# One store of a DMA-bound batched matrix product cut into eight uneven parts

## Chip, cores, metric

The kernel runs on one core of a Trainium2 chip. The metric is the device time of one execution in microseconds (us), lower is better. A "ratio" below is the mean time of one kernel's fast runs over the mean of the fast runs of the kernel before that are recorded with it, so it is not quite the ratio of the medians quoted beside it.

## The reference

```python
# x: 32 x 256 x 512, y: 32 x 512 x 384, float32
def reference(x, y):
    return np.einsum('bij,bjk->bik', x, y).astype(np.float32)
```

In and out together are 54.5 MB, read and written once.

## The kernel before

Batches go in pairs: 16 units u of two batches. Per unit the kernel loads y (two DMAs of 128 rows of 6 KB) and, every second unit, x (128 rows of 16 KB); it transposes x on TensorE, rounds both to float16, multiplies, copies the result to SBUF and stores it with one DMA of 128 rows of 6 KB. All 56 DMAs are issued by SyncE (SP) on one queue.

```python
def store(u):
    keep(nc.sync.dma_start(
        out=out[u * G : (u + 1) * G].rearrange("g (m e) k -> (g m) e k", e=NE),
        in_=o_of.pop(u),                    # tile [128, 4, 384] float32
    ))

for s in range(U + 2):                      # U = 16 units
    if s + ahead < U: load(s + ahead)       # ahead = 2
    # ... (transposes of the first x)
    if s >= 2:        collect(s - 2)        # PSUM -> SBUF copies on ACT and DVE
    if 1 <= s <= U:   multiply(s - 1)
    if s < U:         round_y(s)
    # ... (transposes of the next x)
    if s >= 2:        store(s - 2)
```

`keep` holds the issues in this order on SP. The DMAs take eight completion semaphores in turn, called lanes below: the reports in the trace of the kernel before fall on eight semaphores, 112 on each, 16 for each of seven DMAs. A lane is used again eight DMAs later, and the issue of that DMA waits until the earlier one has landed: the load issued at 104.27 us came 0.02 us after the store of 86.46, eight DMAs before it, had landed. In the kernel's source there is no trace of this: it stands in the instruction list and in the waits of the profile.

## Time and profile before

| | before |
|---|---|
| median of 3 runs | 135.97 us |
| span of the profiled run | 134.3 us |
| DMA queue, share of 16 engines | 97.8% |
| issues of stores 11, 12, 13, 14, 15 | 111.2, 115.9, 123.7, 126.5, 129.1 us |
| last landing | 129.08 + 4.4 = 133.4 us |

Landings are the times at which the 16 DMA engines report to a DMA's semaphore. The trace has each, without the engine's number (the views print only the last of the 16; the others are read from the packed trace itself). Store 11 is reported between 124.03 and 126.00 us, so the engines are up to 2 us apart by then.

The following two views of the kernel before are for comparison with later ones: the DMA view of 124 to 135 us, in 40 slices of 0.275 us, busy share in tenths and GB/s; and the stretch sums (span, busy time of PE, PEld, DVE, ACT and POOL, then clock, DMA share, GB/s).

```profile
DMA  9999999999999999999868999999743100000000
GB/s 425 425 402 402 469 380 439 425 402 425 380 380 469 425 380 447 402 425 402 335 268 335 425 402 447 447 380 402 291 201 156 75 0 0 0 0 0 0 0 0
```

```profile
124.00:125.90 1.90, 1.90 (x27) 1.65 (x24) 1.15 (x4) 1.90 (x6) 0.00 (x0) 1.00 1.04 426
```

The engines are full until 129.2, a few wait for store 15 in three slices, and from slice 28 (131.7) they run dry one by one. Store 12, the one that the change cuts, moves in the first half of this view, at 426 GB/s.

### The profile page before, as it was taken

What the parts mean: (1) busy time and instruction counts of PE and PEld (TensorE: products, weight loads), DVE (VectorE), ACT (ScalarE), POOL (GpSimd) and SP (SyncE); (2) the same over time, 40 slices, a digit from 0 to 9 for tenths busy, and PEclk for the clock granted to TensorE, in tenths of its full rate; (3) what the DMA queues carried; (4) which work ended last, traced back from release to release, by engine and by line L of the source; (5) the groups of instructions that cost most, each with busy time, mean ns of one, the idle gap of its engine ahead of it and who ended that gap; (6) DMA issues with size and microseconds to landing.
All of it is one profiled execution on the core that took longest, in us unless ns stands there. A gap on an engine that the chain in (4) does not pass through costs nothing.

```text
span 134.3 us, 1968 instructions
## 1 busy us (share of the span) xinstructions
PE 88.5 (66%) x768; PEld 73.2 (55%) x768; DVE 56.2 (42%) x128; ACT 63.9 (48%) x129; POOL 0.7 (1%) x6
## 2 busy tenths in 40 slices
PE   0049494979299767786099771976439986597920
PEld 0049474768177666666078661864427665476810
DVE  0004717471743365711634318460363425628620
ACT  3004837662762476712744428560475336738610
POOL 2000000000000000000000000000000000000000
PEclk9999999999959999999968999999965899779997
DMA  5999999999999999999999999999999999999993
GB/s 112 415 400 450 409 417 421 456 388 421 417 448 408 409 428 421 457 394 417 413 443 436 408 417 428 442 422 402 425 423 444 426 402 427 419 427 419 417 394 158
DMA packets 8073, 54.65 MB, mean 407 GB/s; under 512 B 896, under 2 KB 896, under 8 KB 7040
## 3 DMA queue, kind: packets, MB, share of 16 engines
q1 hardware_dynamic: 8064, 54.53, 97.8%
q8 instruction: 6, 0.10, 0.3%
q14 instruction: 3, 0.02, 0.0%
HBM read 41.94 MB, written 12.58 MB: 406 GB/s over the span
## 4 chain that ended last, share of the span: by engine, by line
DMA 78%; PE 13%; ACT 4%; DVE 0%; issue 0%
DMA y_sb<-in_y_dram 40%; DMA x_sb<-in_x_dram 38%; PE o_ps L130 9%; PE t_ps L99 3%; ACT xt_sb L107 2%; ACT y_r L116 1%; ACT o_sb L143 1%; DVE o_sb L145 0%
## 5 line engine op out<-in xcount | busy, mean ns | idle before, releaser
L130 PE MATMUL o_ps<-y_r,xt_sb 128*64 128x384 f16 x512 | 52.4, 364 | 28.5 <-ACT o_sb L143 20.8
L130 PEld LDWEIGHTS <-xt_sb 128*64 128x64 f16 x512 | 39.1, 121 | 38.8 <-issue 22.4
L116 ACT CAST y_r<-y_sb 128x384 f16<-128x384 f32 x64 | 29.5, 514 | 38.7 <-DMA y_sb<-in_y_dram 38.6
L99 PE MATMUL t_ps<-identity,x_sb 128*128 128x128 f32 x256 | 36.9, 301 | 11.4 <-DMA x_sb<-in_x_dram 11.4
L99 PEld LDWEIGHTS t_ps<-identity,x_sb 128*128 128x128 f32 x256 | 34.1, 211 | 16.0 <-issue 16.0
L118 DVE CAST y_r<-y_sb 128x384 f16<-128x384 f32 x64 | 20.0, 356 | 46.7 <-DMA y_sb<-in_y_dram 46.7
L107 ACT CAST xt_sb<-t_ps 128x512 f16<-128x512 f32 x32 | 22.4, 731 | 23.6 <-PE t_ps L99 23.6
L105 DVE CAST xt_sb<-t_ps 128x512 f16<-128x512 f32 x32 | 22.6, 728 | 24.1 <-PE t_ps L99 23.8
L145 DVE COPY o_sb<-o_ps 128x384 f32<-128x384 f32 x32 | 16.3, 544 | 2.1 <-PE o_ps L130 2.1
L143 ACT COPY o_sb<-o_ps 128x384 f32<-128x384 f32 x32 | 13.9, 492 | 1.3 <-PE o_ps L130 1.3
L107 ACT ACT_TABLE_LOAD x1 | 1.3, 1283 | 0.7 <-PEq L192 0.7
masks.py:199 POOL TENSOR_SCALAR_AFFINE_SELECT identity<-identity 128x128 f32<-128x128 f32 x1 | 0.3, 294 | 0.1
masks.py:197 POOL MEMSET identity<- 128x128 f32 x1 | 0.2, 206 | 0.3 <-POOLq L192 0.3
L192 POOL MEMSET const-bfloat16-1.0<- 128x1 bf16 x1 | 0.1, 102 | 0.0
L192 POOL MEMSET const-uint8-127<- 128x1 uint8 x1 | 0.1, 102 | 0.0
L192 POOL MEMSET const-float32-0.0<- 128x1 f32 x1 | 0.1, 99 | 0.2 <-issue 0.2
L192 POOL MEMSET const-float32-1.0<- 128x1 f32 x1 | 0.1, 99 | 0.0
## 6 DMA issues: line engine op xcount, KB each, us to landing
y_sb<-in_y_dram SPq DMA_DIRECT2D x32, 768.0 KB, 17.9
x_sb<-in_x_dram SPq DMA_DIRECT2D x8, 2048.0 KB, 20.8
out_dram<-o_sb SPq DMA_DIRECT2D x16, 768.0 KB, 17.8
```

The source lines that it names most:

```text
L99: nc.tensor.transpose(t_ps[:, f, h], x_sb[:, h * NE + e + f, t::NJ], identity)
L105: keep(nc.vector.tensor_copy(dst, t_ps))
L107: keep(nc.scalar.copy(dst, t_ps))
L116: keep(nc.scalar.copy(yr_of[u][:, g, t], y_sb[:, g, t]))
L118: keep(nc.vector.tensor_copy(yr_of[u][:, g, t], y_sb[:, g, t]))
L130: nc.tensor.matmul(o_ps[g * M : (g + 1) * M], xt_sb[:, t, e, a * PQ : (a + 1) * PQ].rearrange("c p h -> c (p h)"), y_r[:, g, t], start=(t ...
L143: keep(nc.scalar.copy(o_of[u][:, e], ps_of[u][e]))
L145: keep(nc.vector.tensor_copy(o_of[u][:, e], ps_of[u][e]))
L192: nc = _bacc.Bacc("TRN2", target_bir_lowering=False, num_devices=1)
```

## The change

The intent: engines that are late at the end should get fewer rows of one store, early ones more. An unsplit store gives eight to each (eight packets between two reports of an engine, in the kernel before).

```diff
+PARTS = (0, 64, 76, 88, 100, 112, 120, 124, 128)
 ...
     def store(u):
-        keep(nc.sync.dma_start(out=..., in_=o_of.pop(u)))
+        o_sb = o_of.pop(u)
+        dst = out[u * G : (u + 1) * G].rearrange("g (m e) k -> (g m) e k", e=NE)
+        cuts = PARTS if u == U - 4 else (0, P)
+        for k, m in enumerate(cuts[:-1]):
+            rows = slice(m, cuts[k + 1])
+            keep(nc.sync.dma_start(out=dst[rows], in_=o_sb[rows]))
```

(The removed call is shortened.)

More of the change, by code (lines that the diff above doesn't have):

```diff
@@ L148, in store @@
     def store(u):
-        keep(
-            nc.sync.dma_start(
-                out=out[u * G : (u + 1) * G].rearrange("g (m e) k -> (g m) e k", e=NE),
-                in_=o_of.pop(u),
-            )
-        )
+        o_sb = o_of.pop(u)
[4 more added lines that the diff above has]
+            keep(nc.sync.dma_start(out=dst[rows], in_=o_sb[rows]))
     ahead = LAG - 2
```

## The prediction

> **What bounds the kernel now.** I read the page first (the DMA row of the slices, the queue table, the chain of waits), then the waits and the timeline of the engine that issues the DMAs (SP), then the DMA view and the stretch sums of the last ten microseconds.
>
> ```profile
> DMA  5999999999999999999999999999999999999993
> ...
> q1 hardware_dynamic: 8064, 54.53, 97.8%
> ...
> DMA 78%; PE 13%; ACT 4%; DVE 0%; issue 0%
> ```
>
> The first line is the mean busy share of the 16 DMA engines in 40 slices: full from the second slice to the last but one. The second says that the one hardware queue's packets fill 97.8% of 16 engines' span. The third says that the chain that ended last is 78% DMA. PE is busy 66% of the span, ACT 48%, DVE 42%, so the bound is the transport of 54.5 MB, and only the edges can be bettered: time in which some DMA engine is without work. At the end there is some. The sums of three late stretches (columns: span, busy time of PE, PEld, DVE, ACT, POOL, then clock, DMA share, GB/s):
>
> ```profile
> 129.50:130.10 0.60, 0.00 (x0) 0.00 (x0) 0.00 (x0) 0.00 (x0) 0.00 (x0) 1.00 0.74 307
> 130.10:131.50 1.40, 0.00 (x0) 0.00 (x0) 0.00 (x0) 0.00 (x0) 0.00 (x0) 1.00 1.03 426
> 131.50:134.30 2.80, 0.00 (x0) 0.00 (x0) 0.00 (x0) 0.00 (x0) 0.00 (x0) 0.71 0.24 97
> ```
>
> Compute has ended. From 129.5 to 130.1 a quarter of the engines idle, and after 131.5 the share is 0.24. The DMA view of 128.5 to 134.3, with slices of 0.145 us, has the shape:
>
> ```profile
> DMA  8989887759999999999999764535200000000000
> ```
>
> The dip in slices 7 to 9 (129.5 to 129.95) is engines that have ended the last store but one and wait for the last one. From slice 22 (131.7) they run dry one after another until slice 30 (132.9). So the 16 engines are not level: the first is about 1.2 us ahead of the last. That unevenness is what the change goes for. If the engines ended together, the end would come earlier by the unused time after 131.5, that is (132.95 - 131.5) - 0.24 x 2.8 = 0.78 us, plus the dip, 0.26 x 0.6 = 0.16 us: an estimate of 0.9 us at most, 0.7% of the time.
>
> The end itself is set by the last stores. The timeline of the issuing engine in narrow windows, one line each (start, duration, what):
>
> ```profile
> 96.91 0.34 SPq L150 DMA_DIRECT2D out_dram<-o_sb  x1
> 98.71 0.33 SPq L81 DMA_DIRECT2D y_sb<-in_y_dram  x1
> 109.28 0.33 SPq L81 DMA_DIRECT2D y_sb<-in_y_dram  x1
> 111.22 0.34 SPq L150 DMA_DIRECT2D out_dram<-o_sb  x1
> 115.90 0.34 SPq L150 DMA_DIRECT2D out_dram<-o_sb  x1
> 123.67 0.33 SPq L150 DMA_DIRECT2D out_dram<-o_sb  x1
> 126.49 0.33 SPq L150 DMA_DIRECT2D out_dram<-o_sb  x1
> 129.08 0.33 SPq L150 DMA_DIRECT2D out_dram<-o_sb  x1
> ```
>
> The last five are stores 11 to 15 (of 0 to 15). The DMA view gives the time from issue to landing as 14.8, 11.9, 6.0, 5.0 and 4.4 us, so they land at 126.0, 127.8, 129.7, 131.5 and 133.45: 1.83 us apart, the pace of the engines, 0.23 us for one 6 KB row. Store 12 has about ten microseconds of queued work ahead of it. And the waits of the issuing engine:
>
> ```profile
> SPq L150 <- DVE o_sb L145: 20.3, 5, 7.1
> SPq L150 <- DMA y_sb<-in_y_dram: 16.7, 11, 1.6
> SPq L81 <- DMA out_dram<-o_sb: 7.2, 5, 1.4
> ```
>
> A store that waits for a load of y, and a load of y that waits for a store, share no data. The program's instruction list explains it: DMAs take eight completion semaphores in turn ("lanes"), and each issue waits until the DMA eight places earlier has landed. The trace agrees: the load issued at 104.27 came 0.02 us after the store of 86.46, eight DMAs before it, landed (17.8 us later). In the tail this binds nothing today: stores 12 to 15 wait on lanes that came free at 113.0 (issued at 95.02, 18.0 to landing), 114.9, 116.7 and 118.6, long before their data was ready. It is the number that the change disturbs.
>
> [...]the issue at 129.08 ending the dip at about 129.95, 0.8 to 0.95 us.[...]
>
> **The change, part by part.** Removed: one issue of 128 rows. Added: eight issues of 64, 12, 12, 12, 12, 8, 4 and 4 rows, same bytes. On PE, ACT, DVE and POOL the instruction lists are unchanged.
>
> [...]
>
> *Issue time.* Seven more issues by 0.34 us are 2.4 us of SP, which has 7.1 us without work between 116 and 123.67: hidden in themselves.
>
> *Lanes.* This is the part that I think decides. The eight parts take all eight lanes once, and each must wait for what its lane held. Part 0: 115.90. Part 1: lane free at 114.9, issue 116.3. Part 2: 116.7. Part 3: 118.6. Part 4 waits for store 10 (issued 102.46, 18.0): 120.45. Part 5 waits for the y load of 104.27: 122.3. Part 6 waits for the last load (109.28 + 14.8): 124.1. Part 7 waits for store 11: 126.0. Store 13 then takes the lane of part 0. Part 0 stands behind store 11 on every engine, so its last engine ends four rows later: 126.0 + 4 x 0.23 = 126.92. So store 13 goes out at 126.95 and not at 123.67, 3.3 us later, although its data lie ready. Store 14 follows 0.4 us later, store 15 at 129.08 as now.
>
> *What this does to the engines.* Ahead of store 13 they have only store 11 and the parts. The packets of store 11 end at about 123.6 to 125.55 (landings less 0.45 us, the lag between the last packet at 132.95 and the landing at 133.4).[...] Most are therefore dry before store 13's first row reaches them at 126.95 + 0.8 to 0.95 = 127.75 to 127.9. From there nothing is left but three stores: 3 x 1.85 = 5.55, to 133.45, plus 0.45 to land: 133.9. Before it is 133.4 to 133.45. So the levelling is replaced by a common late start, 0.5 us later than the present end.[...] Sum: 135.97 + 0.5[...]: 136.5.
>
> **The rivals.** (a) *Levelling works as meant*: parts all get out early, or the late store 13 costs nothing, and the end moves up to 0.9 us forward: 135.1 to 135.6. For it: the tail's unevenness is real. Against: the queue of eight lanes, which the waits show at work; a DMA issued at 126.95 can't move data before.[...] (c) *Neither*: hidden, 135.9 to 136.0. For that the first row of store 13 would have to arrive by 127.4, half a microsecond after part 0 lands; the one idle start in the trace took 0.8 or more.[...]
>
> **Range and chances.** The shift lies between -0.9 and +0.7[...], and two per cent is 2.7 us. So "within 2%" has nearly all: 0.97; faster 0.01[...]. Predicted 136.5 us. The range, 136.05 to 136.85, holds the shift between +0.1 and +0.9, with 0.1 us of scatter as the three runs before show.
>
> **What would show it.** In the changed profile, the waits of the issuing engine should have a store that waits for a store, and store 13 should be issued near 126.95, store 14 near 127.4, store 15 at 129.1. The DMA row should dip between about 126 and 127.8, and there should be no dip at 129.7. The last landing should be near 133.9, with the engines running dry nearly together. A store 13 near 123.7, or no dip, shows the lane step wrong; a first row less than 0.5 us after the issue shows the latency wrong[...].

The sum is 135.97 + 0.5 = 136.47 us; with a little for a late engine with more rows, 136.5. The +0.7 of the range was rival (b); the chance, 0.02 for slower, was rival (d). That most engines are dry before store 13 is still an estimate from the trace: store 11's packets end at 123.6 to 125.55, and eight rows on average, 1.85 us, end by 127.4, before 127.75. The four rows of part 0 behind store 11 were shown only afterwards: one engine of the changed run updates the semaphore of store 11 at 124.07 us and, four rows on, that of part 0 at 125.00.

## The result and the profile after

The changed kernel takes 136.88 us (median of 4 runs, 136.68 to 137.01) against 136.03 us (4 runs), ratio 1.0057 with a 95% interval of 1.0032 to 1.0082: within 2%, and slower. Five more rounds (changed_again, below) gave 137.43 against 136.06 us, ratio 1.0086 (1.0063 to 1.0109).

The page of the changed kernel, which shows the DMA row, the queue and the chain as the prediction showed them of before:

```profile
DMA  4999999999999999999999999999999999999595
...
q1 hardware_dynamic: 8128, 54.53, 97.4%
...
DMA 78%; PE 12%; ACT 4%; DVE 0%; issue 0%
```

The bound is the same. The one new thing is a 5 in slice 37 of the DMA row, 124.9 to 128.3 us. The DMA view of 124 to 135 us shows it closer:

```profile
DMA  9988986655620088999998999999999999800000
GB/s 425 425 358 313 417 335 246 246 201 201 209 89 22 0 357 357 469 402 492 402 380 358 424 424 380 492 402 380 358 469 424 424 447 380 357 0 0 0 0 0
```

From slice 6 (125.65) the engines run out of work; in slice 13 (127.6) nothing moves at all. In slice 14 all start again, and they stay full to slice 34 (133.6) and stop together. The ragged end of the kernel before, slices 28 to 31, is gone, and so is its dip at 129.5. The hole has moved to the front of store 13 and grown. In stretch sums:

```profile
126.00:127.90 1.90, 1.90 (x28) 1.25 (x23) 0.62 (x2) 0.82 (x2) 0.00 (x0) 1.00 0.35 131
127.90:133.60 5.70, 0.27 (x4) 0.00 (x0) 0.56 (x1) 0.14 (x1) 0.00 (x0) 0.85 1.02 414
```

For 1.9 us the engines were used for 0.35 of their time. What they waited for is in the waits of SP from 115 to 129 us (waiting engine and line, releaser: us in total, times, longest):

```profile
SPq L156 <- DVE o_sb L147: 5.1, 2, 4.2
SPq L156 <- DMA y_sb<-in_y_dram: 4.2, 3, 1.6
SPq L156 <- DMA out_dram<-o_sb: 3.8, 3, 1.6
```

The kernel before, in 115 to 129.2 us, has nothing but waits for data here:

```profile
SPq L150 <- DVE o_sb L145: 15.9, 4, 7.1
SPq L150 <- ACT o_sb L143: 0.3, 1, 0.3
```

The second and third line of the changed kernel are stores that wait for loads and for other stores, that is for lanes. The timeline of SP, in narrow windows, has the issues of stores 13, 14 and 15:

```profile
127.08 0.36 SPq L156 DMA_DIRECT2D out_dram<-o_sb  x1
127.55 0.36 SPq L156 DMA_DIRECT2D out_dram<-o_sb  x1
128.83 0.33 SPq L156 DMA_DIRECT2D out_dram<-o_sb  x1
```

Store 13 goes out 3.4 us later than before (123.67). The DMA issued at 115.98 is part 0; the DMA view gives its size and its time to landing:

```profile
out_dram<-o_sb SPq DMA_DIRECT2D x1, 384.0 KB, 11.0
```

It lands at 127.0, and the issue of store 13 follows. Its first rows start at 127.94, 0.86 us after the issue. The last landing is at 134.16 us, 0.73 us after that of before; the spans differ by 0.78 us (135.05 and 134.27).

### The profile page after: what moved, and what is told of

It is laid out like the page before. It is cut to its first block, busy times and chain, and to the rows that moved or that the text cites. A ratio compares the mean times of both kernels' runs of the same rounds, so it can differ in the third digit from the quotient of the medians.

```text
span 135.0 us, 1975 instructions
## 1 busy us (share of the span) xinstructions
PE 89.1 (66%) x768; PEld 72.8 (54%) x768; DVE 56.3 (42%) x128; ACT 64.0 (47%) x129; POOL 0.7 (1%) x6
## 4 chain that ended last, share of the span: by engine, by line
DMA 78%; PE 12%; ACT 4%; DVE 0%; issue 0%
DMA y_sb<-in_y_dram 40%; DMA x_sb<-in_x_dram 37%; PE o_ps L132 9%; PE t_ps L101 3%; ACT xt_sb L109 2%; ACT y_r L118 1%; ACT o_sb L145 1%; DVE o_sb L147 0%
## 5 line engine op out<-in xcount | busy, mean ns | idle before, releaser
L132 PE MATMUL o_ps<-y_r,xt_sb 128*64 128x384 f16 x512 | 53.5, 369 | 29.3 <-ACT o_sb L145 21.5
L101 PE MATMUL t_ps<-identity,x_sb 128*128 128x128 f32 x256 | 36.4, 299 | 9.8 <-DMA x_sb<-in_x_dram 9.8
L101 PEld LDWEIGHTS t_ps<-identity,x_sb 128*128 128x128 f32 x256 | 33.6, 211 | 14.4 <-issue 14.4
```

What stands on the lines that cost most here:

```text
L101: nc.tensor.transpose(t_ps[:, f, h], x_sb[:, h * NE + e + f, t::NJ], identity)
L132: nc.tensor.matmul(o_ps[g * M : (g + 1) * M], xt_sb[:, t, e, a * PQ : (a + 1) * PQ].rearrange("c p h -> c (p h)"), y_r[:, g, t], start=(t ...
```

## The experiments

Three theories had to be told apart:

- *Lanes*: part 0 holds the lane of store 13, which is therefore issued late.
- *Rows*: a late engine has more rows than before.
- *Close rows*, formed after the second set of runs: rows of one part lie in neighbouring partitions, and engines that read them at the same time slow one another. This was a guess; what led to it is said at eight_16.

Each kernel was timed over five rounds against the kernel before, in three sets and one single run: the first two sets on chip 13, the third on chip 15, the last run on chip 8 (the record names no chip for the first result). The second set shares eleven of its twelve runs of the kernel before with the first. Edits are shown shortened. The rows per engine are counted in the trace for before and changed. For the rest they are an estimate from the engines' reports, the packets under 512 B on the pages: before has 896, so 880 without store 12, and six_parts has 936, 56 more (16 + 12 + 12 + 8 + 4 + 4), heavy_low 912, 32 more (16 + 4 + 12), eight_16 1008, 128 more (8 x 16). "Store 13" is the time of its issue in the profiled run, "end" the last landing there.

| kernel | DMAs of store 12 | rows per engine | store 13, us | end, us | ratio (95%) |
|---|---|---|---|---|---|
| before | 1 | 8 | 123.67 | 133.43 | 1 |
| changed, first result | 8 | 11/9/8/4 | 127.08 | 134.16 | 1.0057 (1.0032-1.0082) |
| changed_again | 8 | 11/9/8/4 | 127.81 | 134.87 | 1.0086 (1.0063-1.0109) |
| six_parts | 6 | 11/9/8/4 | 124.51 | 134.27 | 1.0059 (1.0024-1.0095) |
| level_eight | 8 | 8 | 127.12 | 134.80 | 1.0086 (1.0059-1.0112) |
| lead_96 | 8 | 8 | 127.45 | 134.53 | 1.0109 (1.0079-1.0138) |
| six_again | 6 | 11/9/8/4 | 124.97 | 133.98 | 1.0083 (1.0051-1.0115) |
| level_six | 6 | 8 | 124.61 | 134.47 | 1.0076 (1.0055-1.0098) |
| heavy_low | 3 | 21/4/4/3 | 122.37 | 137.88 | 1.033 (1.0306-1.0354) |
| eight_16 | 8 | 8 | 126.66 | 134.26 | 1.0057 (1.0037-1.0077) |
| col_six | 6, by columns | 8 | 124.58 | 133.62 | 1.0020 (1.0007-1.0033) |
| col_eight | 8, by columns | 8 | 127.04 | 134.09 | 1.0053 (1.0039-1.0067) |
| eight_step8 | 8 | 8 | 126.57 | 133.80 | 1.0052 (1.0034-1.0070) |
| last_halves | 1 (store 15 in 2) | 8 | 123.66 | 133.35 | 1.0012 (0.9993-1.0031) |

### First set: lanes against rows

**changed_again** is the changed kernel without an edit.

> The changed kernel once more, for a comparison on one chip with the three others. Both theories: ratio to the kernel before 1.005 to 1.007, store 13 issued near 127.0 us, the engines dry for a while before 127.9.

Slower than expected, 1.0086. The profile shows why it can vary:

```profile
127.81 0.36 SPq L156 DMA_DIRECT2D out_dram<-o_sb  x1
```

In this run one engine reported store 11 at 126.73, 0.6 us after the next to last (126.10), and part 0 at 127.73. Store 13 is issued 0.08 us after the last of the 16 engines has reported part 0 (127.81 after 127.73 here, 127.08 after 127.00 in the first profile), so the lateness of that one engine went into the start of store 13 on all of them, and the end is 0.71 us later than in the first profile.

**six_parts**:

```diff
-PARTS = (0, 64, 76, 88, 100, 112, 120, 124, 128)
+PARTS = (0, 64, 100, 112, 120, 124, 128)
```

> The same rows on each engine (11, 9, 8 and 4), but in six DMAs of 64, 36, 12, 8, 4 and 4 rows, so that store 13 takes the lane of the last load of y (free near 124.2) and not that of the first part. Lane theory (the late issue of store 13 costs the time): store 13 is issued at 124.2, no dip before it, and most of the loss goes; ratio 0.999 to 1.003[...]. Row theory (11 rows[...] cost the time): the loss stays, ratio 1.005 to 1.007.

Store 13 is early, as planned (timeline of SP):

```profile
124.51 0.36 SPq L156 DMA_DIRECT2D out_dram<-o_sb  x1
```

And the engines stay full (DMA view, 124 to 135 us):

```profile
DMA  9999899899899999999999999999743210000000
```

Yet the ratio, 1.0059, is no better than the change's. So the late issue is not the only thing that can cost this much. In this run the last part but one, of 4 rows, was reported by four engines, at 126.34, 126.42, 127.23 and 128.50: one of these four was the latest of all, and it had, by the estimate in the table, three rows too many. The end stays ragged and comes later: the landings of the last store lie between 132.05 and 134.27 us, before between 132.15 and 133.43.

**level_eight** keeps eight DMAs and 64 rows in front, but gives each engine the same:

```diff
+PIECES = (   # rows, columns
+    (0, 64, 0, 1536), (64, 80, 0, 1536), (80, 96, 0, 1536), (96, 112, 0, 1536),
+    (112, 128, 0, 384), (112, 128, 384, 768), (112, 128, 768, 1152), (112, 128, 1152, 1536))
...
+        for m0, m1, c0, c1 in pieces:
+            keep(nc.sync.dma_start(out=dst[m0:m1, c0:c1], in_=src[m0:m1, c0:c1]))
```

> Store 12 in eight DMAs again, the first with 64 rows as in the change, but level: 8 rows' worth on every engine (then three times 16 rows, and the last 16 rows in four quarters of their columns). Lane theory: store 13 is issued near 127.0 as in the change, and the ratio is 1.004 to 1.007. Row theory: no engine has more than before, ratio 0.999 to 1.002.

Store 13 at 127.12, ratio 1.0086: the loss is there with no uneven row. This speaks for lanes, and against uneven rows as a necessary cause.

**lead_96** is the same with 96 rows in the first DMA, then 16, then six pieces of 256 columns of the last 16 rows.

> Level and in eight DMAs, but the first has 96 rows (6 on each engine), then 16 rows, and the last 16 rows in six pieces of their columns. Lane theory: the first part lands two rows, 0.46 us, later than in the change, store 13 is issued near 127.5, and the end comes 0.46 us later than with the level eight parts: ratio 1.008 to 1.010. Row theory: 0.999 to 1.002.

Timeline of SP, first of level_eight, then of lead_96:

```profile
127.12 0.35 SPq L167 DMA_DIRECT2D out_dram<-o_sb  x1
```

```profile
127.45 0.35 SPq L167 DMA_DIRECT2D out_dram<-o_sb  x1
```

Store 13 is 0.33 us later, since part 0 landed at 127.37 and not at 127.04. Fifteen of the 16 engines report the last store at 134.02 to 134.20 in level_eight, and all 16 at 134.34 to 134.53 in lead_96: again 0.33 us later. (The 0.46 us expected took the two rows for the whole difference; store 11 was also reported 0.09 us earlier here.) The ratios, 1.0086 and 1.0109, go the same way but their intervals overlap. In level_eight the sixteenth engine was 0.6 us behind the rest, at 134.80, after a fetch of instructions of 16 KB had begun on one engine at 127.08 and taken about 1 us. That this engine is the one is likely, not shown: the trace has no engine numbers.

### Second set: what the six parts still cost

**six_again** repeats six_parts, for a comparison in this set.

> The six DMAs of 64, 36, 12, 8, 4 and 4 rows once more, beside the level six on one chip: ratio 1.002 to 1.007, with store 13 issued near 124.2 to 124.6 us; it scatters with which engine happens to be late[...].

1.0083, above the expectation.

**level_six** has six DMAs, level: 64, 16, 16, 16 rows, and the last 16 rows in two halves of their columns.

> Store 12 in six DMAs with 8 rows' worth on every engine (64 rows, three times 16, and the last 16 in two halves of their columns): neither the lane wait nor uneven rows. If the loss of the six parts came from the uneven rows, this has none: ratio 0.999 to 1.002. If splitting the store into six costs by itself (issues, extra completions, a later queue), it is 1.003 to 1.006 as with the uneven six.

This was the surprise. Neither the lane wait (store 13 at 124.61) nor an uneven row, and 1.0076. The expectation had an alternative, that splitting costs by itself; but what in it? Two things showed. First, the stretch in which the parts move (compare 1.04 and 426 GB/s before):

```profile
124.00:125.90 1.90, 1.90 (x26) 1.65 (x24) 1.75 (x6) 1.90 (x6) 0.00 (x0) 1.00 1.02 372
```

The engines are as busy as before and move an eighth less. Some rows take 0.4 to 1.5 us and not the usual 0.234 (the median in the kernel before). From the landings of store 11 to those of store 12 an engine takes 2.35 us on average; before, 1.85. Second, in the DMA view of 131 to 135.5 us the end of the row is one engine working alone:

```profile
DMA  5959697969699714202010100100000000000000
```

The fetch of instructions began late here (127.19; in the kernel before 125.71), and the latest landing moved by 2.65 us from store 12 to store 13, where a store takes 1.85. These 0.8 us of the profiled run are no cost of the split as such; five of the six runs were at 137.15 to 137.4 us and one at 136.56, so it may be that they came in five. The slow rows are then about 0.4 us of a loss of about 1.2 us. What decides the time and the engine of that fetch stays open.

**heavy_low** measures rows by a large dose, 68 of them in one part:

```diff
+PARTS = (0, 48, 116, 128)
```

> Three DMAs of 48, 68 and 12 rows and no lane wait[...]. If rows[...] lengthen the end, by 1.5 to 3.0 us[...]: ratio 1.011 to 1.023. If the end does not depend on how rows are spread (only on lanes), 0.999 to 1.003.

The ratio is 1.033, above the range. The DMA view of 124 to 135 us shows few engines at work at the end:

```profile
DMA  9989999995689999997755999999743323221111
```

The 68-row part was reported by four engines only, at 128.57, 128.62, 129.72 and 132.10. So these 68 rows ran on four engines, 17 on each; and surplus rows on an engine do lengthen the end (137.88 us, before 133.43). With the 48-row and the 12-row part the four have 21 rows by the estimate in the table, thirteen more than before, which is 13 x 0.234 = 3.0 us; the expectation's 1.5 to 3.0 us came from this count. The excess over the 3.0 us of thirteen rows: the latest engine of all reported the 48-row part at 127.07. If it is the one that reported the 68-row part at 132.10, its 17 rows took 5.03 us or 0.296 us each, against the 0.234 us of a row alone, which makes 1.05 us more; and at store 11 the latest engine already reported 0.39 us later than in the kernel before (126.39 and 126.00). Single rows of 0.4 to 0.7 us stand in this stretch too.

**eight_16**: eight DMAs of 16 rows, so that part 0 is done after one row.

```diff
+PARTS = (0, 16, 32, 48, 64, 80, 96, 112, 128)
```

> Eight DMAs of 16 rows, level. The first part is one row per engine and lands 0.24 us after store 11, so store 13 is issued near 126.4 us and not 127.1, and reaches the engines near 127.3. Lane theory: 0.6 to 0.7 us better than the level eight with 64 rows in front; ratio 1.000 to 1.004. If it were the mere count of eight DMAs: 1.006 to 1.009.

Store 13 came at 126.66, between the two theories' times, and the ratio is 1.0057: better than level_eight by 0.3% and not by the 0.5% expected, with intervals that overlap. The last part, issued at 126.22, told what was missing. All 16 engines began its one row between 127.04 and 127.6, and these rows took 0.4 to 0.9 us. The DMA view of 127.02 to 127.50 us:

```profile
DMA packets 20, 0.09 MB, mean 192 GB/s; under 512 B 5, under 2 KB 5, under 8 KB 20
```

And the stretch sum, with the DMA share last but one:

```profile
127.02:127.50 0.48, 0.48 (x10) 0.42 (x7) 0.12 (x1) 0.19 (x1) 0.00 (x0) 1.00 1.38 192
```

Packets count where they begin. Twenty began, five of them semaphore updates, so 15 rows: 1.38 x 16 x 0.48 us = 10.6 us over 15 is 0.71 us for a row, three times the usual. (One of the 15, of 0.234 us, belongs to the part before; the 16 rows of the last part average 0.73 us.)

The rows of this part lie in 16 neighbouring partitions. That their closeness slows them was the guess. No run before this tested it. The third set does.

### Third set: close rows

**eight_step8** is eight_16 with every eighth partition in a part, so that its 16 rows lie eight partitions apart:

```diff
-                rows = slice(m, cuts[k + 1])      # parts of neighbouring rows
+            for k in range(8):
+                keep(nc.sync.dma_start(out=dst[k::8], in_=o_sb[k::8]))
```

> Eight DMAs of 16 rows like the earlier level run, but each takes every eighth partition[...]. [...]the rows that took 0.65 to 0.9 us where all engines started the last part together take about half, 0.4 to 0.5 us, and the ratio falls a little under that run's 1.0057, to 1.002 to 1.005. If the long rows come from the start after idling[...], they stay at 0.65 to 0.9 us.

The rows of the last part, in the DMA view of 127.09 to 127.40 us:

```profile
DMA packets 18, 0.10 MB, mean 317 GB/s; under 512 B 2, under 2 KB 2, under 8 KB 18
```

And in the stretch sum:

```profile
127.09:127.40 0.31, 0.31 (x8) 0.27 (x5) 0.31 (x1) 0.00 (x0) 0.00 (x0) 1.00 1.14 317
```

Sixteen rows in 1.14 x 16 x 0.31 us = 5.65 us: 0.35 us each, half of 0.71 and nearer the undisturbed 0.234. Rows eight partitions apart, half the time: the theory of close rows passes its test, and a slow start after idling alone is out, since the engines had idled here too. Two things stay open. Neighbouring rows of a part are neighbours in DRAM as well, and every eighth row is not; no run varies the partitions alone, so a cause on the DRAM side is not excluded. And why close rows are slow is not shown; single rows took up to 1.49 us (level_six) and 1.57 us (level_eight). The kernel's time hardly moves (1.0052 after 1.0057, different sets): the engines then wait for store 13 in any case.

**col_six** cuts by columns, six DMAs of all 128 rows, so that no part is confined to neighbouring partitions:

```diff
+PIECES = tuple((0, 128, 256 * i, 256 * i + 256) for i in range(6))   # rows, columns
```

> Six DMAs of all 128 rows and a sixth of the columns each: as many DMAs as the level six, no lane wait for store 13, level[...]. [...]rows longer than 0.3 us go from the tail and the ratio is 0.998 to 1.003. If it comes from having six DMAs at all, 1.005 to 1.009 as before.

The first ratio is for the case that close rows made level_six slow, the second for its six DMAs.

Store 13 is early and no lane hole follows (timeline of SP, then the DMA view of 124 to 135 us):

```profile
124.58 0.33 SPq L165 DMA_DIRECT2D out_dram<-o_sb  x1
```

```profile
DMA  9989999999998759999999547999999620000000
```

The ratio is 1.0020, against 1.0076 for level_six in the set before, on another chip. Only two 6 KB rows in its tail (118 to 131 us) took over 0.3 us, where level_six has 13 and the kernel before one, and store 12 took 1.94 us per engine on average. So six DMAs by themselves cost some 0.2%, of which 0.1 us is seen in the latest engine's store 12 (1.92 us, before 1.82).

**col_eight** is the cleanest test here of the lane wait: level, all 128 rows in each part, eight DMAs, the first with half the columns as part 0 of the change has half the rows.

```diff
+c = (0, 768, 896, 1024, 1152, 1280, 1408, 1472, 1536)
+PIECES = tuple((0, 128, a, b) for a, b in zip(c, c[1:]))             # rows, columns
```

> Eight DMAs cut by columns (half of them in the first, then five times 128 columns and twice 64): level[...], only the lane wait of the change. Lane theory: store 13 issued near 127.0 us, first rows near 127.9, the ratio 1.003 to 1.006. If the lane wait costs nothing by itself[...]: 0.998 to 1.002.

Timeline of SP, then the DMA view of 124 to 135 us:

```profile
127.04 0.33 SPq L167 DMA_DIRECT2D out_dram<-o_sb  x1
```

```profile
DMA  9999997565742099999999999999999999600000
```

The hole of the changed kernel is back, in the same place (slices 6 to 13 of 124 to 135 us), and the end is level. The ratio is 1.0053, against 1.0020 for col_six of the same set and chip. So the lane wait costs 0.33%, 0.45 us; the slowest run of col_six (136.57 us) is faster than the fastest of col_eight (136.73). The two differ also in the number and the widths of the parts, but that is not what sets the end: all 16 engines begin store 13 at 127.87 to 128.01, after its late issue at 127.04, and no 6 KB row in this tail takes over 0.3 us.

### A last run

**last_halves** asks whether the idle time of the early engines at the end of the kernel before is worth anything: store 12 whole, and the last store in two halves of its columns, the first issued when its copies are done.

> Store 12 is whole again; instead the last store, 15, goes out in two halves of its columns, the first when its two copies are done, about 1.2 us before the whole store went. It fills the dip of the kernel before in which a quarter of the engines waited for the last store (0.16 us on average). If the end is set by the latest engine, which never waited, nothing moves: ratio 0.999 to 1.001. If the idle engines counted: 0.998 or less.

1.0012 (0.9993 to 1.0031): nothing gained. The first half went out at 127.77, and the early engines report the second at 131.53 and not at 132.15; the latest still reports at 133.35 (133.43 before). No kernel here beats the kernel before.

## Why the prediction was right

The direction, the class and the mechanism held. The predicted 136.5 us is 0.4 us under the median of 136.88, which is 0.03 us over the upper end of the range; 135.97 times the ratio of 1.0057 is 136.75, inside it. That the number came so close is in part luck: with the 1.0086 of changed_again, where one engine was late, it would be 137.14, outside. By its steps:

- *Rows per engine*. The semaphores of the parts were updated by 12, 8 and 4 engines, beside one update from the issuing engine. Which engines they were the trace does not number.
- *The lanes.* Right, and the core of it. Issues of parts 0 to 7 predicted (and measured): 115.90 (115.98), 116.3 (116.59), 116.7 (117.22), 118.6 (118.65), 120.45 (120.53), 122.3 (122.36), 124.1 (124.22), 126.0 (126.09). Part 0 lands 126.92 (127.00), store 13 126.95 (127.08), store 14 127.4 (127.55), store 15 129.1 (128.83). col_eight shows that this wait suffices for 0.45 us, without the uneven rows and the close rows of the change.
- *First rows 0.8 to 0.95 us after the issue.* Right: 0.86, though the reading behind it was not: the dip in the prediction's view is slices 6 to 8, 129.37 to 129.80 us, and not 129.5 to 129.95. By that end of the dip it would have been 0.72 us.
- *Three stores in 5.55 us.* This term was too small. (The landings of stores 11 to 15 are 1.86 us apart on average, not 1.83; the 1.85 of the sum is near that.) From the first row at 127.94 to the last semaphore packet at 133.8 it is 5.87 us. All engines now work in step, and a row takes 0.2404 us on average from there on, where it took 0.2358 from 120 us to the end in the kernel before; 24 rows by 4.6 ns are 0.11 us. The first rows start over 0.15 us (127.94 to 128.08), so as much of the 5.87 is the difference of the first engine's start and the last one's end. What is left is under 0.1 us.
- *Rival (b), a late engine with more rows*. Not on the path of the profiled run, where all engines waited for store 13. It shows as soon as the lane wait is gone, in six_parts and heavy_low.
- *The intent: the four engines without a 12-row part should be the late ones.* Not so in this run: these four reported part 0 at 125.44, 125.46, 125.80 and 125.82, by matching the landings of parts 0 and 1, against a mean of 125.93 for all. The four latest, 126.59 to 127.00, were among the other twelve, where no row was taken off. In changed_again the matching puts the latest engine among the four without a 12-row part. Which engine is late changes from run to run.
- *What I didn't see*: that neighbouring rows cut out of a store can move more slowly than in the whole (0.71 us each in the last part of eight_16, 0.35 with every eighth row, 0.234 in the kernel before). Such a split has a price of its own, 0.4 us per engine in level_six (2.35 us for store 12, against 1.94 in col_six). In the changed kernel it is hidden, by little: the last row of the parts ended at 127.75 us, the first row of store 13 began at 127.94. This fits six_parts, where taking the lane wait away brought nothing back; how much of the loss there is slow rows and how much surplus rows (0.7 us for three) was not separated.

So the time of the changed kernel is set by the late issue of store 13. Behind it stands a second cost, slow or surplus rows in the parts, which shows when the first is removed (six_parts, six_again and level_six, 1.0059 to 1.0083). Their sum is not the loss; the later of the two is.

## What to carry to other kernels

Before splitting a DMA, count what each piece takes besides bytes: here a completion semaphore that the DMA eight places later has to wait for, until the slowest of 16 engines has reported (in the changed kernel this moved an issue from 123.67 to 127.08 us). If it must be split, a cut along the columns, with all 128 rows in each piece, was the cheaper one here (1.0020 in col_six, 1.0076 in level_six). And when one suspect is removed and nothing comes back, look for a second cost under it before acquitting the first: two kernels that both lack the second cost and differ in the first (col_six and col_eight) settled what the first removal could not.
